# mLSTM heads' ends: squares ahead of the output gate, a root table asked for ahead of its use, and a sixth out-projection tile beside the last head

## The chip, the cores and the metric

The kernel runs on one core of one Trainium2 chip. The metric is the device time of one launch in microseconds (us). The engines are named as in the profile: PE (TensorE, matrix multiplies; its weight loads are PEld), DVE (VectorE), ACT (ScalarE), POOL (GpSimd) and SP (SyncE, which issues most weight loads). Each runs its own instructions in a fixed order and waits on semaphores for the others. What lies in PSUM, where matmuls add up, has names that begin with `p` (`pmm`, `psc`, `ptr`, of which there are three, three and two).

## The reference, cut to what matters

The kernel computes two layers of an encoder on 512 tokens of width 1024. The change lies in the first layer's mixer: four mLSTM heads of width 192 and a memory attention are set side by side, multiplied by one matrix, and added to the input:

```python
hm = mlstm_chunkwise(q, k, v, ig, jax.nn.log_sigmoid(fg))      # num / max(|den|, exp(-m)) per head
hm = hm * lax.rsqrt(jnp.mean(hm * hm, axis=-1, keepdims=True) + EPS)
hm = hm.reshape(bsz, seq, A_WIDTH) * a_head_g[a]
mix_out = (hm * jax.nn.sigmoid(o)).astype(x.dtype)
mem_out = memory_attention(q_mem, mem, mem_w_kv[l])
x = x + jnp.concatenate([mix_out, mem_out], axis=-1) @ a_w_out[a]
x = x + conv_ffn(rmsnorm(x, norm_ffn_g[l]), ...)
```

## The kernel before

All activations lie transposed, 128 features by 512 tokens in a tile. Every float32 operand of a matmul is split into a high part (`split` casts it, ACT, L113) and a low part (the difference, DVE, L114), and each product is three matmuls (`mm3`, L157 to L159: high by high, low by high, high by low in the weights). Weights come from memory in `wr` (SP), and are split into `wh` and `wl`; there are three buffers of each.

`mlstm_head(h)` is a generator. For each of the four blocks of 128 keys it makes weighted scores (the exp of a gate term on ACT, L1136; the scores on PE; their product on DVE, L1142; split to `pt`), and `products` multiplies them by the values into two `ptr` tiles. Then comes the head's end: both tiles are squared on ACT (L1172) and multiplied by the output gate `og` on DVE (L1174); the denominator's floor is added to the squares (L1177, L1178), the sum is split, summed over the features by a matmul with ones (L1186), and a reciprocal square root on ACT (L1188, with its table load, since it lies in another table than exp) with one Newton step on DVE (L1189 to L1191) gives the factor. The gated tiles are multiplied by it (L1194) and split: these are the mixes of the head, operands of the out-projection. Heads 0 to 2 fill mixes 0 to 3 in part, head 3 the mixes 4 and 5; the memory attention gives 6 and 7.

`weave(job, filler, each)` interleaves: for each `yield` of the job (or each unit of `yield 2.6`), `each` steps of the filler are taken. For heads 0 to 2 the filler is projections of the layer's input, for head 3 the out-projection's steps, one `mm3` a step. A scheduler then orders each engine's instructions by its own estimates, so the code's order is not the program's order.

`OutProjection` has the eight output tiles in groups: tiles 0 to 2 in `pmm`, 3 and 4 in `ptr`. `part(g, ks)` loads the weights of group g for the mixes ks and issues one `mm3` for each mix and tile. `finish` goes through all eight tiles: one that no group holds is made by `project` on the spot (24 matmuls, weights of 512 KB), then the residual is added (DVE, L609), the tile written out, its square added up (ACT L245 or L248, DVE L249) and the scaled tile split for the feed-forward network (ACT L285, DVE L286). Its weights follow.

Of the kernel before, what the change touches and what calls it, by code (L numbers as in the profile page):

```python
# [12 lines left out]
AF = mybir.ActivationFunctionType  # L13
ALU = mybir.AluOpType
AX = mybir.AxisListType

P = 128
# [6 lines left out]
AH = 4  # L24
# [22 lines left out]
def f(ap):  # L47
    return ap.bitcast(F32)
# [3 lines left out]
def trunk(  # L52
# [19 lines left out]
    V, A, G = nc.vector, nc.scalar, nc.gpsimd  # L72
# [10 lines left out]
    def sb(tag, shape, dtype=F32):  # L83
        count[0] += 1
        return pool.tile(shape, dtype, tag=tag, name=f"{tag}{count[0]}", bufs=bufs[tag])

    def ps(tag):
        count[0] += 1
        return psum.tile([P, S], F32, tag=tag, name=f"p{tag}{count[0]}", bufs=pbufs[tag])

    def small(n=4):
        return sb("s", [P, 32])[:, :n]
# [4 lines left out]
    ones = cpool.tile([P, P], F32, name="ones")  # L97
# [7 lines left out]
        out=maskf, in_=maskf, pattern=[[1, P]], base=0, channel_multiplier=-1,  # L105
# [6 lines left out]
    def split(hi, lo, src, on_act=True, pinned=False):  # L112
        high = A.copy(hi, src) if on_act else V.tensor_copy(hi, src)  # L113
        low = V.tensor_tensor(out=lo, in0=src, in1=f(hi), op=ALU.subtract)  # L114
        if pinned:
            pin(high)
            pin(low)
# [37 lines left out]
    def mm3(o, lh, ll, rh, rl, first, last, more=False):  # L155

        nc.tensor.matmul(o, lh, rh, start=first, stop=False, skip_group_check=more)  # L157
        nc.tensor.matmul(o, lh, rl, start=False, stop=False, skip_group_check=more)  # L158
        nc.tensor.matmul(o, ll, rh, start=False, stop=last, skip_group_check=more)  # L159
# [13 lines left out]
    def run(gen):  # L173
        while True:
            try:
                next(gen)
            except StopIteration as end:
                return end.value

    def chain(*gens):  # L180
        for g in gens:
            yield from g
# [6 lines left out]
    def weave(job, filler, each, lead=0):  # L189

        due = lead
        for n in chain([0], job):
            due += each if n is None else each * n
            while due >= 1:
                due -= 1
                next(filler, None)
# [293 lines left out]
    def head_scores(o, h, q, tsl, k, c, first, keys_first=False):  # L490

        for i, part in enumerate(q):
            a, b = part[h][:, tsl], k[h][:, c]
            if keys_first:
                a, b = b, a
            nc.tensor.matmul(o, a, b, start=first and i == 0, stop=i == 1)  # L496
# [479 lines left out]
    e, u, c, r = (cpool.tile([P, TT, AH], F32, name=f"gate{i}") for i in range(4))  # L976
# [76 lines left out]
    mixes = [None] * KT  # L1053
# [28 lines left out]
    qs, ks, og = [None] * 6, [None] * 6, [None] * 6  # L1082

    def a_tiles(*js):
        for j in js:
            qs[j] = yield from qk_tile(j)
            ks[j] = yield from qk_tile(6 + j)
        for j in js:
            og[j] = yield from o_tile(j)
# [8 lines left out]
    def exponents(h, s):  # L1098

        n = S - s * P  # L1100
        r = sb("bias", [P, S])
        src = bass.AP(tensor=rowd.tensor, offset=rowd.offset + (s * AH + h) * S + s * P, ap=[[0, P], [1, n]])
        pin(G.dma_start(r[:, :n], src))
        exps[h, s] = r
# [3 lines left out]
    def den_floor(h):  # L1108

        floors[h] = sb("bias", [P, S])  # L1110
        src = bass.AP(tensor=floord.tensor, offset=floord.offset + h * S, ap=[[0, P], [1, S]])
        pin(G.dma_start(floors[h], src))
# [11 lines left out]
    def mlstm_head(h):  # L1124
        hp, odd = divmod(h, 2)
        sh = 3 * hp + 1
        full = 3 * hp + 2 * odd
        rs, ds = HEADS[odd], HEADS[1 - odd]
        pt = sb("pt", [P, 5 * S], F32R)

        def weighted_scores(s):
            n = S - s * P
            sl = slice(s * P, (s + 1) * P)
            r = exps.pop((h, s))
            e = sb("t", [P, S])
            A.activation(e[:, :n], r[:, :n], AF.Exp, bias=acol[:, s, h : h + 1])  # L1136
            yield
            o = ps("sc")
            kf, qf = ks[full], qs[full]
            mm3(o[:, :n], kf[0][:, sl], kf[1][:, sl], qf[0][:, s * P :], qf[1][:, s * P :], True, False)  # L1140
            head_scores(o[:, :n], odd, qs[sh], slice(s * P, S), ks[sh], sl, False, True)
            V.scalar_tensor_tensor(e[:, :n], o[:, :n], DH**-0.5, e[:, :n], op0=ALU.mult, op1=ALU.mult)  # L1142
            split(pt[:, RO[s] : RO[s + 1]], pt[:, 1280 + RO[s] : 1280 + RO[s + 1]], e[:, :n])
            yield

        nums = []

        def products(s):
            if not nums:
                nums.extend(ps("tr") for _ in range(2))  # L1150
            for o, c in zip(nums, (3 * P, 2 * P) if odd else (0, P)):
                mm3(
                    o[:, s * P :], vh[hp][s][:, c : c + P], vl[hp][s][:, c : c + P],
                    pt[:, RO[s] : RO[s + 1]], pt[:, 1280 + RO[s] : 1280 + RO[s + 1]], s == 0, s == TT - 1,
                )
            yield

        yield from weighted_scores(0)
        yield from weighted_scores(1)
        yield from weighted_scores(2)  # L1160
        yield from products(0)
        yield from weighted_scores(3)
        den_floor(h)
        for s in range(TT if h < AH - 1 else 0):
            exponents(h + 1, s)
        yield from products(1)
        yield from products(2)
        yield from products(3)
        sqs = []
        for o, j, r in ((nums[0], full, slice(0, P)), (nums[1], sh, rs)):  # L1170
            sq = sb("t", [P, S])
            A.activation(sq, o, AF.Square)  # L1172
            sqs.append(sq)
            V.tensor_tensor(out=og[j][r, :], in0=o[r, :], in1=og[j][r, :], op=ALU.mult)  # L1174
        yield
        sq, den = sqs
        V.scalar_tensor_tensor(den[ds, :], den[ds, :], EPS * DH / HD, floors.pop(h)[ds, :], op0=ALU.mult, op1=ALU.max)  # L1177
        V.tensor_add(sq, sq, den)  # L1178
        hi, lo = sb("t", [P, S], F32R), sb("t", [P, S], F32R)
        split(hi, lo, sq)  # L1180
        for s in range(TT if h < AH - 1 else 0):
            masked(h + 1, s)
        yield 2.6
        o = ps("sc")
        for i, part in enumerate((hi, lo)):
            nc.tensor.matmul(o, onesr, part, start=i == 0, stop=i == 1)  # L1186
        fb, t = sb("t", [P, S]), sb("t", [P, S])
        A.activation(fb, o, AF.Abs_reciprocal_sqrt, scale=1.0 / DH)  # L1188
        V.tensor_mul(t, fb, fb)  # L1189
        V.scalar_tensor_tensor(t, t, -0.5 / DH, o, op0=ALU.mult, op1=ALU.mult)  # L1190
        V.scalar_tensor_tensor(fb, t, 1.5, fb, op0=ALU.add, op1=ALU.mult)  # L1191
        yield 3.4
        for j, r in ((full, slice(0, P)), (sh, rs)):
            V.tensor_tensor(out=og[j][r, :], in0=fb[r, :], in1=og[j][r, :], op=ALU.mult)  # L1194
            if mixes[j] is None:
                mixes[j] = sb("u", [P, S], F32R), sb("u", [P, S], F32R)
            split(mixes[j][0][r, :], mixes[j][1][r, :], og[j][r, :])

    outp = OutProjection(a_w_out, mixes, (0, 3, "mm"), (3, 5, "tr"))
    run(value_columns(1))  # L1200
    load_vectors(1)
    load_vectors(2)
# [2 lines left out]
    fill = gate_rows()  # L1205
# [6 lines left out]
    fill = chain(a_tiles(2), a_memory_queries(0), a_tiles(3, 4), a_tiles(5), a_memory_queries(1))  # L1212
# [10 lines left out]
    fill = chain(outp.part(0, 0, 1), outp.part(0, 2, 6), outp.part(0, 3))  # L1223
    weave(memory_attention(memq[1], memkv, 1, mixes), fill, 0.475)
    job = mlstm_head(3)
    fill = chain(fill, outp.part(0, 7))
    weave(islice(job, 13), fill, 0.85)
    fill = chain(fill, outp.part(1, 0, 1, 2, 6), outp.part(1, 3, 7))
    weave(job, fill, 0.862)
    run(chain(fill, outp.part(0, 4, 5), outp.part(1, 4, 5)))  # L1230
    norm, (act,) = outp.finish([col["gffn"][:, 0:8]])


# [19 lines left out]
    for j in range(KT):  # L1253
        wh, wl = weights(rows(ffn_w_down[0], j * P, P, FT - LAST, FT), LAST, P)
        o = ps("mm")
# [10 lines left out]
    mixes = [None] * KT  # L1266
# [98 lines left out]
    outp = OutProjection(b_w_out, mixes, (0, 3, "mm"), (3, 5, "sc"))  # L1365
    fill = chain(*(project_pair(j) for j in range(5)), b_memory_queries(0), project_pair(5), b_memory_queries(1))
# [11 lines left out]
    fill = chain(outp.part(0, 0, 1), outp.part(0, 2, 6), outp.part(0, 3, 4))  # L1378
    weave(memory_attention(memq[1], memkv, 1, mixes), fill, 0.48, 4)
    job = band_attention(5, *qkv.pop(5))  # L1380
    fill = chain(fill, outp.part(0, 7))
    weave(islice(job, 8), fill, 2.372)
    fill = chain(fill, outp.part(1, 0, 1, 2, 6), outp.part(1, 3, 4, 7))
# [124 lines left out]
```

## Time and profile before

| | |
|---|---|
| three runs | 1206.86, 1205.56, 1205.6 us; median 1205.6 |
| profiled execution | 1206.7 us, span 1204.9 us, granted PE clock 0.998 in the mean |
| busy: PE, DVE, ACT, POOL | 1185.9, 940.3, 723.1, 145.1 us |
| matmuls `pmm<-u,wh` and `pmm<-u,wl` of 128x512 on L157 to L159 | 968 on each line, 336.3, 333.6 and 333.4 us |
| the stretch 240 to 260 us (head 3's end, out-projection) | PE busy 17.45 of 20.00 us, granted clock 0.91 |
| the stretch 260 to 280 us | PE busy 20.00 of 20.00 us, granted clock 1.00 |

A row of the timeline gives the start in the span, the duration, engine, line, operation, output and inputs, the shape, how many of a kind follow one another, and in brackets the idle time ahead of it with the work that ended it. A matmul's duration includes its fill, so rows overlap; the distance of starts tells the pace. A row of the waits gives who waited for whom, us in total, times, and the longest. A row of a window gives its length, busy time and instructions, the granted clock as a share of full speed, the DMA engines' share and GB/s.

### The profile page before, as it was taken

The numbers are of one execution on the slowest core, as the hardware profiler recorded it, in microseconds if no ns is written. First come the engines' busy times: TensorE is split into PE (matmuls) and PEld (weight loads), VectorE is DVE, ScalarE is ACT, GpSimd is POOL, SyncE is SP. The second block draws the span as 40 slices with busy tenths as digits, with TensorE's granted clock in tenths as the row PEclk, the third lists the DMA queues.
The fourth block names the chain that finished last, engine by engine and source line by source line (L and its number), as shares of the span: only waits on it lengthen the run. The fifth ranks groups of instructions, "written<-read, shape, count | busy, mean of one in ns | idle before, by whom it ended". The sixth has DMA issues, their size and how long they took to land.

```text
span 1204.9 us, 18596 instructions
## 1 busy us (share of the span) xinstructions
PE 1185.9 (98%) x6963; PEld 1048.4 (87%) x6963; DVE 940.3 (78%) x1666; ACT 723.1 (60%) x1266; POOL 145.1 (12%) x234
## 2 busy tenths in 40 slices
PE   9999999999999999999999999999999999999997
PEld 9988888877889999999888888888888999999986
DVE  6877797777978777777698888997896777777755
ACT  4547796654656555555566677775565555555545
POOL 0202201011011111111020000101101010111100
PEclk9999999999999999999999999999999999999999
DMA  8637322448465777665563313244745466666551
GB/s 277 204 103 163 94 73 71 144 139 191 108 155 139 161 163 160 150 145 126 140 205 119 88 56 98 74 141 150 183 105 132 118 130 139 140 141 136 119 157 70
DMA packets 206635, 162.83 MB, mean 135 GB/s; under 512 B 8420, under 2 KB 186058, under 8 KB 206546
## 3 DMA queue, kind: packets, MB, share of 16 engines
q1 hardware_dynamic: 184338, 120.78, 34.2%
q0 software_dynamic: 22208, 40.87, 18.1%
q8 instruction: 54, 0.88, 0.3%
q14 instruction: 35, 0.29, 0.1%
HBM read 133.09 MB, written 32.47 MB: 137 GB/s over the span
## 4 chain that ended last, share of the span: by engine, by line
PE 80%; issue 12%; DVE 2%; DMA 2%; ACT 2%; POOL 1%; POOLq 0%; SPq 0%; ACTq 0%; DVEq 0%
PE pmm L157 15%; PE pmm L159 15%; PE pmm L158 15%; PE ptr L158 5%; PE ptr L157 5%; PE ptr L159 5%; PE psc L159 5%; PE psc L157 4%; PE psc L158 4%; PE psc L496 2%; DMA pt<-in_ffn_w_up_dram 2%; PE ptr L1335 1%; POOL xspill L610 1%; ACT wh L113 0%; PE ptr L1356 0%
## 5 line engine op out<-in xcount | busy, mean ns | idle before, releaser
L157 PE MATMUL pmm<-u,wh 128*128 128x512 f32 (+1 forms) x968 | 336.3, 348 | 2.2 <-ACT u L113 2.1
L158 PE MATMUL pmm<-u,wh 128*128 128x512 f32 (+1 forms) x968 | 333.6, 345 | 0.0
L159 PE MATMUL pmm<-u,wl 128*128 128x512 f32 (+1 forms) x968 | 333.4, 345 | 0.0
L114 DVE TENSOR_TENSOR wl<-wr,wh 128x1024 fp32r<-128x1024 f32 (+4 forms) x168 | 194.5, 1158 | 96.5 <-ACT wh L113 95.5
L113 ACT CAST wh<-wr 128x1024 fp32r<-128x1024 f32 (+4 forms) x168 | 167.9, 1000 | 93.9 <-PE pmm L158 44.5
L157 PEld LDWEIGHTS pmm<-u,wh 128*128 128x128 f32 x968 | 183.9, 190 | 21.2 <-ACT u L113 3.1
L159 PEld LDWEIGHTS pmm<-u,wl 128*128 128x128 f32 x968 | 183.9, 190 | 21.1
L158 PEld LDWEIGHTS pmm<-u,wh 128*128 128x128 f32 x968 | 184.1, 190 | 18.2 <-DVE u L114 0.2
L157 PE MATMUL ptr<-u,wh 128*128 128x512 f32 x272 | 106.8, 394 | 0.0
L158 PE MATMUL ptr<-u,wh 128*128 128x512 f32 x272 | 106.5, 392 | 0.0
L159 PE MATMUL ptr<-u,wl 128*128 128x512 f32 x272 | 105.8, 389 | 0.0
L727 POOL DMA_DIRECT2D xspill<-t x64 | 56.0, 875 | 408.1 <-ACT t L726 399.0
L157 PE MATMUL pmm<-u,u 128*128 128x256 f32 x296 | 84.5, 285 | 2.8 <-ACT t L803 2.8
L159 PE MATMUL pmm<-u,u 128*128 128x256 f32 x296 | 84.0, 284 | 0.4 <-DVE u L114 0.4
L158 PE MATMUL pmm<-u,u 128*128 128x256 f32 x296 | 83.8, 283 | 0.0
L114 DVE TENSOR_TENSOR u<-pt,u 128x512 fp32r<-128x512 f32 x102 | 69.8, 687 | 9.7 <-ACT u L113 7.1
L726 ACT COPY t<-ptr 128x512 f32<-128x512 f32 x64 | 37.5, 586 | 65.4 <-PE ptr L159 65.4
L157 PE MATMUL psc<-u,wh 128*128 128x256 f32 (+1 forms) x232 | 76.1, 328 | 0.0
L158 PE MATMUL psc<-u,wh 128*128 128x256 f32 (+1 forms) x232 | 75.9, 327 | 0.0
L114 DVE TENSOR_TENSOR u<-t,u 128x512 fp32r<-128x512 f32 x78 | 53.3, 688 | 22.6 <-ACT u L113 22.2
L113 ACT CAST u<-pt 128x512 fp32r<-128x512 f32 x102 | 63.0, 618 | 11.4 <-DVE pt L838 11.2
L900 ACT ACTIVATE t<-t 128x512 f32<-128x512 f32 x34 | 21.5, 633 | 80.2 <-DVE t L636 80.2
(281 smaller groups left out, 2557.2 us busy)
## 6 DMA issues: line engine op xcount, KB each, us to landing
wr<-in_ffn_w_up_dram SPq DMA_DIRECT2D x54, 512.0 KB, 4.4
wr<-in_ffn_w_down_dram SPq DMA_DIRECT2D x38, 512.0 KB, 3.8
pt<-in_ffn_w_up_dram SPq DMA_DIRECT2D x34, 512.0 KB, 6.6
xspill<-t POOLq DMA_DIRECT2D x64, 256.0 KB, 4.9
wr<-in_a_w_in_dram SPq DMA_DIRECT2D x20, 512.0 KB, 3.9
xspill<-u POOLq DMA_DIRECT2D x32, 256.0 KB, 2.9
u<-xspill SPq DMA_DIRECT2D x32, 256.0 KB, 5.1
wr<-in_w_kv_dram SPq DMA_DIRECT2D x12, 512.0 KB, 4.0
```

Of the source, the lines that this page charges most:

```text
L113: high = A.copy(hi, src) if on_act else V.tensor_copy(hi, src)
L114: low = V.tensor_tensor(out=lo, in0=src, in1=f(hi), op=ALU.subtract)
L157: nc.tensor.matmul(o, lh, rh, start=first, stop=False, skip_group_check=more)
L158: nc.tensor.matmul(o, lh, rl, start=False, stop=False, skip_group_check=more)
L159: nc.tensor.matmul(o, ll, rh, start=False, stop=last, skip_group_check=more)
L496: nc.tensor.matmul(o, a, b, start=first and i == 0, stop=i == 1)
L610: pin(G.dma_start(xspill[j], xT[j]))
L726: A.copy(t, o)
L727: G.dma_start(xspill[j], t, accum_op=ALU.add)
L900: A.activation(self.acc, self.acc, AF.Silu)
L1335: nc.tensor.transpose(tp[:, b * P : (b + 1) * P], es[T, h][:, b * P : (b + 1) * P], ident)
```

## The change

In every head the squares of both tiles are issued ahead, and the multiplies by the output gate come behind the split of the sum. The filler ahead of the ones-matmul grows (`yield 3.6` for 2.6). Head 3 computes a reciprocal square root of a column of ones behind its split, whose result nobody reads. The out-projection has a third group, tile 5 alone in `psc`, whose parts for mixes 0, 1, 2, 6, 3 and 7 join the filler of head 3, with 1.4 steps a yield for 0.862, and whose parts 4 and 5 come behind those of the other groups. So `finish` makes tiles 6 and 7 on the spot, where it made 5, 6 and 7. Lines of the changed kernel: L1176, L1177 for the floor and the sum (L1177, L1178 before), L1181 for the gate (L1174), L1185 for the new root, L1189 for the ones-matmul (L1186), L1191 to L1194 for the root (L1188 to L1191), L1197 for the mixes (L1194).

```diff
@@ mlstm_head
-        for o, j, r in ((nums[0], full, slice(0, P)), (nums[1], sh, rs)):
+        for o in nums:
             sq = sb("t", [P, S])
             A.activation(sq, o, AF.Square)
             sqs.append(sq)
-            V.tensor_tensor(out=og[j][r, :], in0=o[r, :], in1=og[j][r, :], op=ALU.mult)
         yield
...
         split(hi, lo, sq)
+        for o, j, r in ((nums[0], full, slice(0, P)), (nums[1], sh, rs)):
+            V.tensor_tensor(out=og[j][r, :], in0=o[r, :], in1=og[j][r, :], op=ALU.mult)
         for s in range(TT if h < AH - 1 else 0):
             masked(h + 1, s)
-        yield 2.6
+        if h == AH - 1:
+            A.activation(small(1), ones[:, :1], AF.Abs_reciprocal_sqrt)
+        yield 3.6
...
-    outp = OutProjection(a_w_out, mixes, (0, 3, "mm"), (3, 5, "tr"))
+    outp = OutProjection(a_w_out, mixes, (0, 3, "mm"), (3, 5, "tr"), (5, 6, "sc"))
...
-    fill = chain(fill, outp.part(1, 0, 1, 2, 6), outp.part(1, 3, 7))
-    weave(job, fill, 0.862)
-    run(chain(fill, outp.part(0, 4, 5), outp.part(1, 4, 5)))
+    fill = chain(fill, outp.part(1, 0, 1, 2, 6), outp.part(1, 3, 7), outp.part(2, 0, 1, 2, 6, 3, 7))
+    weave(job, fill, 1.4)
+    run(chain(fill, outp.part(0, 4, 5), outp.part(1, 4, 5), outp.part(2, 4, 5)))
```

The matmuls are as many as before, 6944. DVE has one instruction more, and ACT four (the new root, one cast more of weights, two table loads more: 27 for 25). On SP one load of 512 KB (the weights of tile 5) becomes eight of 64 KB.

Where the instructions stand now, at four places. First ACT, from the memory attention's last casts (`pt`, L113) to head 3's first exps (L1136). Before:

```order
L553 ACTIVATE t_2395,s_2393<-psc_2368,s_2392 128x256 x2
L113 CAST pt_2324<-ptr_2401 128x2x256
L113 CAST pt_2325<-ptr_2411 128x2x256
L113 CAST pt_2324<-ptr_2418 128x2x256
L113 CAST pt_2325<-ptr_2428 128x2x256
L113 CAST wh_2605<-wr_2600 128x1024
L515 COPY t_2449<-ptr_2435 64x512
L515 COPY t_2449<-ptr_2443 64x512
L1136 ACTIVATE t_2469<-bias_2143,acol 128x512
```

And now:

```order
L113 CAST pt_2325<-ptr_2411 128x2x256
L113 CAST wh_2567<-wr_2565 128x384
L1185 ACT_TABLE_LOAD
L1185 ACTIVATE s_2598<-ones 128x1
L113 CAST pt_2324<-ptr_2418 128x2x256
L113 CAST pt_2325<-ptr_2428 128x2x256
L515 COPY t_2449<-ptr_2435 64x512
L1136 ACT_TABLE_LOAD
L1136 ACTIVATE t_2469<-bias_2143,acol 128x512
L515 COPY t_2449<-ptr_2443 64x512
```

The new root and its table load have moved up into the memory attention, and a load of exp's table follows ahead of the head's scores. Second PE, around head 3's ones-matmuls (`onesr`), with the out-projection's filler about them. Before:

```order
L159 MATMUL ptr_2598<-u_1521,wl_2606 128x512
L1186 MATMUL psc_2615<-t_2594,onesr 128x512
L157 MATMUL ptr_2599<-u_1521,wh_2605 128x512
L158 MATMUL ptr_2599<-u_1522,wh_2605 128x512
L159 MATMUL ptr_2599<-u_1521,wl_2606 128x512
L1186 MATMUL psc_2615<-t_2595,onesr 128x512
```

And now:

```order
L159 MATMUL ptr_2600<-u_1762,wl_2608 128x512
L1189 MATMUL psc_2626<-t_2592,onesr 128x512
L1189 MATMUL psc_2626<-t_2593,onesr 128x512
L157 MATMUL ptr_2601<-u_1762,wh_2607 128x512
L158 MATMUL ptr_2601<-u_1763,wh_2607 128x512
```

The two parts of the sum now follow each other, and fifteen matmuls of filler stand between the head's last products and them, where nine stood ahead of the first. Third PE, where tile 6 (`pmm_2803` before, `pmm_2817` now, with the weights `wh_2799`, `wl_2800` and `wh_2813`, `wl_2814`) begins. Before:

```order
L159 MATMUL pmm_2763<-u_2454,wl_2760 128x512
L157 MATMUL pmm_2803<-u_1516,wh_2799 128x512
L158 MATMUL pmm_2803<-u_1517,wh_2799 128x512
L159 MATMUL pmm_2803<-u_1516,wl_2800 128x512
L157 MATMUL pmm_2803<-u_1521,wh_2799 128x512
```

And now:

```order
L159 MATMUL psc_2671<-u_2655,wl_2749 128x512
L157 MATMUL pmm_2817<-u_1519,wh_2813 128x512
L158 MATMUL pmm_2817<-u_1520,wh_2813 128x512
L157 MATMUL pmm_2857<-u_1519,wh_2853 128x512
L158 MATMUL pmm_2857<-u_1520,wh_2853 128x512
L157 MATMUL pmm_2898<-u_2762,wh_2894 128x512
L158 MATMUL pmm_2898<-u_2763,wh_2894 128x512
L159 MATMUL pmm_2817<-u_1519,wl_2814 128x512
```

Before, tile 5's 24 matmuls (`pmm_2763`) ran ahead of tile 6; now the last six of tile 5 (`psc_2671`), and then the high halves of tile 6, of tile 7 and of the network's first tile (`pmm_2898`). Fourth DVE, the same place. Before, behind the first three residuals:

```order
L609 TENSOR_TENSOR u_2314<-u_2314,ptr_2598 128x512
L609 TENSOR_TENSOR u_2316<-u_2316,ptr_2599 128x512
L114 TENSOR_TENSOR wl_2800<-wr_2797,wh_2799 128x1024
L249 TENSOR_TENSOR rb_2715<-rb_2715,t_2741 128x512
L286 SCALAR_TENSOR_TENSOR u_2745<-u_2314,cols_519,u_2744 128x512
```

And now:

```order
L609 TENSOR_TENSOR u_2314<-u_2314,ptr_2600 128x512
L609 TENSOR_TENSOR u_2316<-u_2316,ptr_2601 128x512
L609 TENSOR_TENSOR u_2318<-u_2318,psc_2671 128x512
L249 TENSOR_TENSOR rb_2760<-rb_2760,t_2786 128x512
L286 SCALAR_TENSOR_TENSOR u_2790<-u_2314,cols_519,u_2789 128x512
L249 TENSOR_TENSOR rb_2760<-rb_2760,t_2795 128x512
L286 SCALAR_TENSOR_TENSOR u_2799<-u_2316,cols_519,u_2798 128x512
L249 TENSOR_TENSOR rb_2760<-rb_2760,t_2804 128x512
L114 TENSOR_TENSOR wl_2814<-wr_2811,wh_2813 128x1024
```

The low half of tile 6's weights stood behind five residuals; it now stands behind six, and behind the norm sums and scalings of tiles 3 and 4 too.

## The prediction

> **What bounds the kernel now.** I read the page's first two parts, the list of waits, and then the timeline of TensorE (PE) over the four heads' ends, with DVE and ACT beside it.
>
> ```profile
> span 1204.9 us, 18596 instructions
> PE 1185.9 (98%) x6963; PEld 1048.4 (87%) x6963; DVE 940.3 (78%) x1666; ACT 723.1 (60%) x1266; POOL 145.1 (12%) x234
> ```
>
> PE is busy for 98% of the span and no other engine for more than 78%. The change leaves the number of matmuls as it was, so it can move the time only by taking holes out of PE's stream or putting new ones in. The profiled execution took 1206.7 us; the three runs have a median of 1205.6, so I sum against 1206.7 and take 1.1 off at the end. What differs from the time before by 0.2%, 2.4 us, or less cannot be told from no change.
>
> What the holes cost is read from starts: PE's rows start one pace apart while it streams.
>
> ```profile
> 259.42 0.39 PE L157 MATMUL pmm<-u,wh 128*128 128x512 f32 x1
> 261.46 0.39 PE L157 MATMUL pmm<-u,wh 128*128 128x512 f32 x1
> ```
>
> Nine rows lie between these two, all of one kind: 2.04 us / 9 = 0.227 us a matmul. A start that comes later than that has lost the excess. The waits that touch the stage of the change:
>
> ```profile
> PE pmm L157 <- ACT u L113: 2.1, 1, 2.1
> PE psc L1186 <- ACT t L113: 1.5, 4, 0.4
> ```
>
> The second is each head's end: the matmul by ones (L1186) waits for the cast of the summed squares. The rows just ahead of each and it:
>
> ```profile
> 128.64 0.39 PE L158 MATMUL pmm<-u,wh 128*128 128x512 f32 x1
> 129.27 0.50 PE L1186 MATMUL psc<-t,onesr 128*128 128x512 f32 x1 [0.24 <-ACT t L113]
> 129.61 0.40 PE L159 MATMUL pmm<-u,wl 128*128 128x512 f32 x1
> ...
> 150.60 0.39 PE L159 MATMUL pmm<-u,wl 128*128 128x512 f32 x1
> 151.43 0.50 PE L1186 MATMUL psc<-t,onesr 128*128 128x512 f32 x1 [0.44 <-ACT t L113]
> ...
> 206.53 0.39 PE L158 MATMUL pmm<-u,wh 128*128 128x512 f32 x1
> 207.28 0.50 PE L1186 MATMUL psc<-t,onesr 128*128 128x512 f32 x1 [0.36 <-ACT t L113]
> ...
> 241.03 0.40 PE L159 MATMUL ptr<-u,wl 128*128 128x512 f32 x1
> 241.87 0.50 PE L1186 MATMUL psc<-t,onesr 128*128 128x512 f32 x1 [0.44 <-ACT t L113]
> ```
>
> Start to start less the pace: 0.40, 0.60, 0.52 and 0.61 us, and the matmul behind starts 0.34 instead of 0.23 after it, 0.11 more each time. So the four ends cost 0.51, 0.71, 0.63 and 0.72 us. Head 3 has the large hole too, where the out-projection needs the last head's mixes:
>
> ```profile
> 248.39 0.39 PE L159 MATMUL ptr<-u,wl 128*128 128x512 f32 x1
> 250.89 1.61 PE L157 MATMUL pmm<-u,wh 128*128 128x512 f32 x3 [2.11 <-ACT u L113]
> ```
>
> The windows (PE's busy time and instructions, granted clock, DMA share, GB/s):
>
> ```profile
> 39.34:42.75 3.41, 1.96 (x11) 1.00 0.35 78
> 42.75:46.16 3.41, 3.37 (x19) 1.00 0.93 266
> 247.55:250.96 3.41, 1.30 (x7) 1.00 0.51 154
> 250.96:254.38 3.42, 3.42 (x8) 0.50 0.51 152
> ```
>
> From 248.39 to 250.89 are 2.50 us, less one pace 2.27 us of wait. Behind the window with 1.30 us of work PE ran 3.42 us at clock 0.50, eight matmuls where fifteen fit, 3.42 - 8 x 0.227 = 1.6 us lost; with the ramp's edges I take 1.7. A window with 1.96 us of work elsewhere was followed by full clock, so the limit lies between the two.
>
> The Trainium skill ("TensorE: Matmul & The Clock Gate", Part 1) puts the drop behind an idle window of some 3.4 us. Here a wait of 2.27 us was enough, in a window that was 38% busy; by the page a new hole of this size would cost no clock, by the row it does, and I go by the row.
>
> **The change part by part.** *Squares ahead, og multiplies behind the split, heads 0 to 2.* The number of DVE operations does not change. The order of the two kernels shows DVE with the same four operations ahead of the cast in heads 0 and 1 and one multiply less in head 2, and PE with the ones-matmul later by 1 matmul (head 0) and 3 (head 1), and two places earlier in head 2, 0.23 us each. One multiply of the gate takes this long:
>
> ```profile
> 148.59 0.69 DVE L1174 TENSOR_TENSOR u<-ptr,u 64x512 f32<-64x512 f32 x1
> ```
>
> Head 0: 0.51 - 0.23, and the low half no longer splits PE's stream, 0.1 left. Head 1: 0.71 - 0.69 for three matmuls, but its low half is due right behind and DVE's taps stand ahead of it, 0.35 left. Head 2: 0.63 - 0.69 + 0.46, 0.45 left. Gain 0.51 + 0.71 + 0.63 - 0.90 = 0.9 (0.95, taken down). Ends: 0.4 if the scheduler's other moves (convolution taps put ahead of the low half in heads 0 and 1) make the low half late, 1.8 if all goes.
>
> *Head 3's root (yield 3.6, denser filler).* The ones-matmul now stands 15 matmuls behind the products instead of 9: 6 x 0.23 = 1.4 us later against a wait of 0.61, and its low half follows directly, due as the DVE row ends.
>
> ```profile
> 241.20 0.62 ACT L113 CAST t<-t 128x512 fp32r<-128x512 f32 x1 [1.21 <-DVE t L1178]
> 241.90 0.69 DVE L114 TENSOR_TENSOR t<-t,t 128x512 fp32r<-128x512 f32 x1
> 243.38 1.28 ACT L1188 ACT_TABLE_LOAD   x1 [1.56 <-PE psc L1186]
> ```
>
> Gain 0.7 (0.4 to 0.72).
>
> *The root's table, "early".* It does not come early in the order. The dummy's load and ACTIVATE (L1185) stand between the memory attention's casts, a third load brings exp back for head 3's scores, and the real root (L1191) still has its own load behind its wait on PE. So the load of 1.28 us at 243.38 stays in the chain and two more are issued, 2.57 us of ACT, in a stretch where it waits now and then:
>
> ```profile
> 226.00 0.59 ACT L113 CAST pt<-ptr 128x512 fp32r<-128x512 f32 x1 [1.42 <-PE ptr L565]
> 230.34 1.63 ACT L1136 ACTIVATE t<-bias,acol 128x512 f32<-128x512 f32 x3
> 231.35 0.39 PE L159 MATMUL pmm<-u,wl 128*128 128x512 f32 x1
> 232.19 0.33 PE L157 MATMUL psc<-u,u 128*128 128x128 f32 x1 [0.46 <-DVE t L1142]
> ```
>
> The scores of head 3 lose 0.84 - 0.23 = 0.61 at 232.19 now, for the exp that started at 230.34. In the new order the exps alternate with the casts they feed, and two filler matmuls more stand ahead of the last score. Walking the queues row by row I get a gain of 0.5 in this stretch; the ends are a gain of 0.9 (such waits gone, the 0.61 and what the casts behind it lose) and a loss of 2.57 (both loads on the path). The Trainium skill ("ScalarE: Activation LUTs", What ACT_TABLE_LOAD costs) has a switch at 2.66 us with its drain; the row has 1.28, and by the page's price, an estimate, this end would be 2.8 us deeper.
>
> *Tile 5 beside head 3.* Its 18 matmuls stand between the ones-matmuls and the first use of a mix. From the low half's start the mixes took 250.89 - 242.91 = 8.0 us, an ACT cast in between that waited for PE included:
>
> ```profile
> 242.91 0.39 PE L1186 MATMUL psc<-t,onesr 128*128 128x512 f32 x1
> 248.63 1.04 ACT L113 CAST wh<-wr 128x1024 fp32r<-128x1024 f32 x1 [2.14 <-PE ptr L158]
> 250.85 1.41 DVE L114 TENSOR_TENSOR u<-u,u 128x512 fp32r<-128x512 f32 x2
> ```
>
> Now 39 matmuls lie between the low half and that use, 39 x 0.227 = 8.8 us. The wait of 2.27 goes and with it the clock drop of 1.7. Gain 4.0; the cover is thin for the second low half, so 3.5 at the lower end.
>
> *What tile 5 no longer covers.* Behind its parts PE now issues three pairs by high halves (tiles 6, 7 and the FFN's first), and then stands at tile 6's low half, `wl_2814`. On DVE that split waits behind the residuals, norm sums and scalings of six tiles; before, behind ten such operations, with tile 5's 24 matmuls to hide them:
>
> ```profile
> 255.99 2.05 DVE L609 TENSOR_TENSOR u<-u,pmm 128x512 f32<-128x512 f32 x3 [3.74 <-PE pmm L159]
> 257.99 0.75 DVE L286 SCALAR_TENSOR_TENSOR u<-u,cols,u 128x512 fp32r<-128x512 f32 x1
> 258.66 0.68 DVE L249 TENSOR_TENSOR rb<-rb,t 128x512 f32<-128x512 f32 x1
> 261.19 1.28 DVE L609 TENSOR_TENSOR u<-u,ptr 128x512 f32<-128x512 f32 x2
> 262.38 1.22 DVE L114 TENSOR_TENSOR wl<-wr,wh 128x1024 fp32r<-128x1024 f32 x1
> ```
>
> From the first residual to that split's start: 262.38 - 255.99 = 6.39 us for 10 operations, 0.64 each and back to back. Now there are 16 (6 + 5 + 5): 10.2 us, and 1.22 for the split: ready 11.45 us after the first residual. PE at that time has 29 matmuls left ahead of the low half (5 of tiles 1 and 2, 12 of tiles 3 and 4, 6 of tile 5, 6 high halves): 29 x 0.227 = 6.6 us. The hole is 4.9 us, in two pieces, since the last of the three pairs waits for ACT's cast behind the same work. Ends: 3.9 if DVE's operations overlap better, 5.5.
>
> A hole of 4.9 us is longer than the window that dropped the clock. Shared evenly by two windows it leaves each at least 2.4 us without work, less busy than the 1.96 us that kept the clock, so I expect a drop. What it costs hangs on the phase: 0.5 if most of the slow window is still hole, 1.7 for one full, 2.2 for one and a part. I take 1.4.
>
> *Loads and the rest.* One load of 512 KB becomes eight of 64 KB on SP; casts of tile 5's weights are now three. They run ahead by three buffers beside PE's fill and cost nothing; if one were late it would be a wait like the row at 248.63, at most its own 1 us. What follows (norm's sums, FFN's weights) depends on PE's and DVE's end here and shifts with them.
>
> Sum: -0.9 - 0.7 - 0.5 - 4.0 + 4.9 + 1.4 = +0.2 us: 1206.9 for the profiled execution, 1205.8 beside the median.
>
> **The rivals.** *As its words say (faster).* The hole at 250.89 goes and none comes: if the split of tile 6 were not late, because DVE had the residuals of the early tiles done while PE streams, the sum would be -6.1: 1199.5. For it speaks that DVE waits 3.74 us ahead of 255.99; against it that no residual can be added before its tile's last mix, so the ten operations cannot move ahead. Between the two lies a smaller hole (3.9) without a clock drop: -0.9 - 0.7 - 0.5 - 4.0 + 3.9 = -2.2, and with 0.4 more from the heads -2.6: 1203.0.
>
> *The table loads land on the path (slower).* The second extra load stands directly ahead of head 3's first exp, and PE waits for the scores made from it already. If ACT has no idle time there to take the two loads, the stretch loses 2.57 us instead of gaining 0.5: +0.2 + 3.1 = +3.3, 1208.9. The idle of 1.42 us before 226.00 speaks against it; it decides from the point where ACT, with the loads, still works on the casts `pt` when PE reaches the first products, some 1.4 us of delay onward.
>
> *The new hole costs two slow windows.* 2.6 instead of 1.4 us: +1.4, 1207.0, within the same bound.
>
> *No drop behind the new hole.* If only a window wholly without work drops the clock, the hole's pieces of about 3.2 and 1.1 us cost none: +0.2 - 1.4 = -1.2, 1204.4, within the same bound. One pair of rows, 247.55 and 250.96, speaks against it and none for it. (This is the rule of the Trainium skill's page on TensorE named above.)
>
> *The table loaded early after all.* If the early load served the root, 1.28 us would leave the mixes' chain; since the 39 matmuls cover that chain anyway, the sum would not change.
>
> **How the numbers follow.** The forecast, a new hole that gives back what the old one cost, has 0.58, the version without a drop (0.1) and that with two (0.1) in it. A smaller hole without a drop, at about 1203, has 0.14; the words' version 0.10 at 1199.5; the loads on the path 0.10 at 1208.9; several terms at their bad ends together 0.08, above that. All good ends of the terms but no missing hole: -1.8 - 0.7 - 0.9 - 4.0 + 3.9 + 0.5 = -3.0, 1202.6; all bad ones: -0.4 - 0.4 + 2.6 - 3.5 + 5.5 + 2.2 = +6.0, 1211.6. The range 1202.0 to 1209.2 takes in the first and reaches to the loads' rival, and leaves out the words' version (0.10) and the worst sums (0.06). Faster by over 0.2% (below 1203.2): 0.24; within: 0.58; slower (above 1208.0): 0.18.
>
> **What would show it.** In the new profile: no wait of `L157 pmm` for ACT's `u` ahead of the mixes and full clock there; head 3's ones-matmul without a wait; 27 table loads, one of them of L1185 among the memory attention's casts; and, as the sign of the forecast, a wait of PE at L159 for DVE's `wl` (and two matmuls ahead of it one at L157 for ACT's cast), 4 to 5 us in all, six high halves behind tile 5's end, with a window of lower clock behind it. If that wait is missing I am wrong by the terms 4.9 and 1.4, and the kernel is faster by 6 us; if PE waits more than now at head 3's scores, by the term 0.5.

## The result, and the profile after

The changed kernel took 1210.54 us in the median of six runs (1209.01 to 1211.74), the kernel before 1206.16 beside it: a ratio of 1.0035 (95% interval 1.0024 to 1.0047), 4.2 us slower, where 0.2 us more was forecast. The profiled execution is the quickest of the six. Its PE has as many instructions as before, 6963.

```profile
span 1207.1 us, 18613 instructions
PE 1187.3 (98%) x6963; PEld 1047.2 (87%) x6963; DVE 940.3 (78%) x1667; ACT 725.1 (60%) x1270; POOL 146.6 (12%) x234
```

The waits of PE that are new or longer, from the list of waits after:

```profile
PE pmm L157 <- ACT wh L113: 4.6, 3, 3.0
PE pmm L159 <- DVE wl L114: 0.9, 1, 0.9
PE psc L1189 <- DVE t L114: 0.5, 2, 0.3
PE ptr L157 <- ACT pt L113: 0.4, 1, 0.4
PE psc L1189 <- ACT t L113: 0.2, 1, 0.2
```

The wait `PE pmm L157 <- ACT u L113` of 2.1 us is gone, the first line has grown from 1.4 us (one wait) to 4.6 (three), and the fourth from 0.2 to 0.4. PE's timeline shows where the largest are, behind the last matmul of tile 5 (`psc`):

```profile
260.69 0.39 PE L159 MATMUL psc<-u,wl 128*128 128x512 f32 x1
260.92 0.49 PE L157 MATMUL pmm<-u,wh 128*128 128x512 f32 x1
261.25 0.40 PE L158 MATMUL pmm<-u,wh 128*128 128x512 f32 x1
261.85 0.50 PE L157 MATMUL pmm<-u,wh 128*128 128x512 f32 x1 [0.21 <-ACT wh L113]
262.19 0.40 PE L158 MATMUL pmm<-u,wh 128*128 128x512 f32 x1
265.58 0.50 PE L157 MATMUL pmm<-u,wh 128*128 128x512 f32 x1 [3.00 <-ACT wh L113]
265.93 0.39 PE L158 MATMUL pmm<-u,wh 128*128 128x512 f32 x1
267.24 0.79 PE L159 MATMUL pmm<-u,wl 128*128 128x512 f32 x1 [0.92 <-DVE wl L114]
267.83 0.63 PE L157 MATMUL pmm<-u,wh 128*128 128x512 f32 x1
```

Seven starts between 260.69 and 267.24 would take 7 x 0.227 = 1.59 us; they take 6.55. The hole is 4.96 us, against 4.9 forecast. The work that it waits for, on DVE:

```profile
255.68 2.05 DVE L609 TENSOR_TENSOR u<-u,pmm 128x512 f32<-128x512 f32 x3 [2.04 <-PE pmm L159]
...
262.07 0.68 DVE L609 TENSOR_TENSOR u<-u,psc 128x512 f32<-128x512 f32 x1
...
265.37 0.68 DVE L249 TENSOR_TENSOR rb<-rb,t 128x512 f32<-128x512 f32 x1
265.97 1.22 DVE L114 TENSOR_TENSOR wl<-wr,wh 128x1024 fp32r<-128x1024 f32 x1
```

From the first residual to the split's start are 265.97 - 255.68 = 10.29 us for 16 operations (forecast 10.2), DVE without a gap. Behind the hole the clock drops, in the windows of that execution (PE busy, granted clock, DMA share, GB/s):

```profile
263.42:266.83 3.41, 0.73 (x2) 1.00 0.49 179
266.83:270.25 3.42, 3.01 (x7) 0.50 0.50 149
270.25:273.66 3.41, 3.41 (x16) 1.00 0.90 257
```

The heads' ends, just ahead of the ones-matmul and at it:

```profile
129.15 0.39 PE L157 MATMUL pmm<-u,wh 128*128 128x512 f32 x1
129.69 0.50 PE L1189 MATMUL psc<-t,onesr 128*128 128x512 f32 x1 [0.15 <-DVE t L114]
...
153.50 0.39 PE L157 MATMUL pmm<-u,wh 128*128 128x512 f32 x1
154.21 0.50 PE L1189 MATMUL psc<-t,onesr 128*128 128x512 f32 x1 [0.31 <-DVE t L114]
...
206.37 0.39 PE L159 MATMUL pmm<-u,wl 128*128 128x512 f32 x1
206.98 0.50 PE L1189 MATMUL psc<-t,onesr 128*128 128x512 f32 x1 [0.22 <-ACT t L113]
```

Less the pace they lose 0.31, 0.48 and 0.38 us, with 0.11 behind each; before it was 0.40, 0.60 and 0.52. In heads 0 and 1 it is now the sum's low half, DVE's, that PE waits for.

To see where all of it went I took from the timelines the start of PE's n-th matmul and subtracted that of the kernel before; both have issued the same number by then, and the start of the stage (the 700th) is taken as zero. A positive number is time lost. In us:

| kernel | behind head 2 (1200th) | behind head 3's products (1255th) | among the mixes (1325th) | in tile 7 and the network's first tile (1400th) |
|---|---|---|---|---|
| changed | +0.77 | +0.73 | -3.76 | +2.75 |
| e3, heads' order only | +0.75 | -0.29 | -0.15 | -0.15 |
| g4, the same with yield 2.6 | +0.37 | -0.66 | -0.73 | -0.73 |
| f3, early root only | -0.02 | +0.70 | -0.15 | -0.15 |
| e4, tile 5 only | -0.03 | -0.04 | -4.05 | +3.01 |
| e2, changed without the early root | +0.72 | -0.31 | -4.71 | +2.95 |
| e1, changed, tiles 6 and 7 first | +0.76 | +0.74 | -3.78 | -3.78 |
| g2, e1 without the early root | +0.79 | -0.26 | -4.63 | -4.63 |

The first column hangs on its place, since the kernels issue the matmuls of this stretch in different orders. From the 1110th to the 1138th, just behind head 2's sum, it would read +0.54 to +0.56 for the changed kernel, +0.51 to +0.53 for e3 and +0.04 to +0.06 for g4; at the 1220th, ahead of head 3's first scores, +0.87, +0.84 and +0.46.

So the changed kernel loses 0.77 over heads 0 to 2 (0.54 to 0.87 by the place), nothing at head 3's products, wins 4.49 at the mixes, and loses 6.51 at the new hole.

### The profile page after: what moved, and what is told of

Same layout as the page of the kernel before. It is cut to its first block, busy times and chain, and to the rows that moved or that the text cites. A ratio compares the mean times of both kernels' runs of the same rounds, so it can differ in the third digit from the quotient of the medians.

```text
span 1207.1 us, 18613 instructions
## 1 busy us (share of the span) xinstructions
PE 1187.3 (98%) x6963; PEld 1047.2 (87%) x6963; DVE 940.3 (78%) x1667; ACT 725.1 (60%) x1270; POOL 146.6 (12%) x234
## 4 chain that ended last, share of the span: by engine, by line
PE 77%; issue 12%; DVE 3%; ACT 3%; DMA 3%; POOL 1%; SPq 0%; POOLq 0%; ACTq 0%; DVEq 0%
PE pmm L157 15%; PE pmm L158 14%; PE pmm L159 14%; PE ptr L157 5%; PE ptr L158 5%; PE ptr L159 5%; PE psc L159 5%; PE psc L157 4%; PE psc L158 4%; DMA pt<-in_ffn_w_up_dram 2%; PE psc L496 2%; PE ptr L1338 1%; POOL xspill L610 1%; DVE t L1063 1%; PE ptr L1359 0%
## 5 line engine op out<-in xcount | busy, mean ns | idle before, releaser
L157 PE MATMUL pmm<-u,wh 128*128 128x512 f32 (+1 forms) x960 | 333.2, 347 | 3.3 <-ACT wh L113 3.2
L114 DVE TENSOR_TENSOR wl<-wr,wh 128x1024 fp32r<-128x1024 f32 (+2 forms) x169 | 194.5, 1153 | 95.9 <-ACT wh L113 95.6
L113 ACT CAST wh<-wr 128x1024 fp32r<-128x1024 f32 (+2 forms) x169 | 167.7, 995 | 100.2 <-PE pmm L158 47.6
L157 PEld LDWEIGHTS pmm<-u,wh 128*128 128x128 f32 x960 | 182.6, 190 | 22.6 <-ACT wh L113 4.3
L157 PE MATMUL ptr<-u,wh 128*128 128x512 f32 x272 | 106.7, 392 | 0.0
L157 PE MATMUL pmm<-u,u 128*128 128x256 f32 x296 | 84.5, 285 | 2.5 <-ACT t L803 2.5
L157 PE MATMUL psc<-u,wh 128*128 128x256 f32 (+1 forms) x240 | 79.2, 330 | 0.0
L158 PE MATMUL psc<-u,wh 128*128 128x256 f32 (+1 forms) x240 | 79.0, 329 | 0.0
L113 ACT CAST u<-pt 128x512 fp32r<-128x512 f32 x102 | 63.0, 617 | 11.7 <-DVE pt L838 11.7
```

## The experiments

Theory A: the loss is the new hole in front of tile 6's low half and the slow clock behind it. Theory B: the two table loads and the new order at the heads cost it.

**e1: tiles 6 and 7 first.** In `OutProjection.finish`:

```diff
             for j in range(KT):
-                o = self.o[j] if j in self.o else run(project(self.w, j * P, self.mixes))
+                if j not in self.o:
+                    self.o[j] = run(project(self.w, j * P, self.mixes))
+            for j in range(KT):
+                o = self.o[j]
                 V.tensor_add(xT[j], xT[j], o)
```

> The changed kernel, with finish issuing the products of tiles 6 and 7 ahead of all residuals, so that tile 6's low half stands behind three residuals on DVE instead of behind sixteen operations. Theory A (the loss is the new hole of 5.0 us in front of tile 6's low half and the slow clock behind it, 1.5 us in the profiled run and more in others): hole and slow window gone, 5 to 8 us less than the changed kernel, 1202.5 to 1205.5, so faster than the kernel before by 1 to 3.5 us. Theory B (the two extra table loads and the new order at the heads' ends cost the time): no more than 1 us less than the changed kernel, 1209 to 1210.5.

1202.6 us in the median of 5 runs, ratio to the kernel before 0.9962 (0.995 to 0.9975): 4.6 us faster, more than the 1 to 3.5 expected. Its DVE and PE at the same place:

```profile
255.50 2.05 DVE L612 TENSOR_TENSOR u<-u,pmm 128x512 f32<-128x512 f32 x3 [2.04 <-PE pmm L159]
257.83 1.22 DVE L114 TENSOR_TENSOR wl<-wr,wh 128x1024 fp32r<-128x1024 f32 x1 [0.28 <-ACT wh L113]
...
260.52 0.39 PE L159 MATMUL psc<-u,wl 128*128 128x512 f32 x1
260.74 0.39 PE L157 MATMUL pmm<-u,wh 128*128 128x512 f32 x1
260.97 0.39 PE L158 MATMUL pmm<-u,wh 128*128 128x512 f32 x1
261.20 0.39 PE L159 MATMUL pmm<-u,wl 128*128 128x512 f32 x1
```

The split follows three residuals instead of sixteen operations and ends at 259.05, two microseconds before PE needs it at 261.20; PE runs through. The residuals and norm sums run beside the 48 matmuls of tiles 6 and 7. The table's last column falls from +2.75 to -3.78: the hole and its clock were 6.5 us of the profiled execution. Theory A holds, theory B alone cannot give this.

**e2: no early root.** The two lines `if h == AH - 1:` and `A.activation(small(1), ...)` out.

> The changed kernel without the root of a column of ones (and so without the two table loads more). Theory A: within 1 us of the changed kernel, 1209.5 to 1211; the hole of 5 us stands. Theory B: 2 to 2.6 us less than the changed kernel, about 1208, and the wait of 0.57 us at head 3's first products gone.

1209.36 us (11 runs), ratio 1.0015 (1.0006 to 1.0024). The median lies between what theory A and theory B expected, 1.2 us below the changed kernel's. The runs alone do not decide between them. In the trace the hole stands, as theory A has it, and the early root's 1.0 us is gone at head 3's products (+0.73 to -0.31). In the table's last column this gain is hidden by the clock, which was at half for two windows behind the hole instead of one.

**e3: the heads' order alone.** The out-projection as before, no early root.

> Only the new order of the heads' ends (squares ahead, gate behind the split, yield 3.6); no new root, no tile 5. Theory A: the wait ahead of the mixes (2.3 us) and its slow window stay as before, the ones-matmul of head 3 gains up to 0.6, heads 0 to 2 nothing: 1205 to 1207. Theory B: slower than before by 1 to 2 us, 1207 to 1208.

1206.83 us (11 runs), ratio 0.9995 (0.9986 to 1.0004). As theory A has it: no measurable difference. It loses 0.75 over heads 0 to 2 and wins 1.04 at head 3's products; the wait ahead of the mixes is there, 2.27 us as before.

**e4: tile 5 alone.** The third group, its parts and the 1.4 steps on top of the kernel before.

> Only the sixth out-projection tile beside head 3 (with 1.4 steps a yield), heads' ends as before. Theory A: the old hole of 2.3 us and its slow window gone, the new hole of 5 us and its slow windows there: like the changed kernel within 1.5 us, 1209 to 1212. Theory B: no extra loads and no new order at the heads, so no slower than before, 1203 to 1206.

1210.07 us (11 runs), ratio 1.0026 (1.0017 to 1.0035). Within the noise the whole loss is there with tile 5 alone. Its windows show the clock at half for two windows on end:

```profile
261.53:264.94 3.41, 1.36 (x5) 1.00 0.32 112
264.94:268.35 3.41, 1.62 (x3) 0.50 0.33 124
268.35:271.77 3.42, 3.42 (x9) 0.50 0.60 175
```

Behind the first, with 1.36 us of work, the second is at half clock; the second has the rest of the hole in it, and behind it the third is at half clock too, in which PE has full work. What the hole costs through the clock thus hangs on how it lies across the windows, and I set out to price that.

**f1 and f2: the hole filled.** f1 is the changed kernel again. In f2 tile 6's first matmul is issued twelve times more, into the same accumulator, which each starts anew; PE has them to do while it would stand idle.

```diff
+        for _ in range(again):
+            nc.tensor.matmul(o, wh[:, 0, :], act[0][0], start=True, stop=False, skip_group_check=True)
         for k in range(n):
             mm3(o, wh[:, k, :], wl[:, k, :], act[k][0], act[k][1], k == 0, k == n - 1)
...
-                o = self.o[j] if j in self.o else run(project(self.w, j * P, self.mixes))
+                o = self.o[j] if j in self.o else run(project(self.w, j * P, self.mixes, again=12 if j == 6 else 0))
```

> The changed kernel once more, for the comparison with the three kernels beside it on the same chip: 1209 to 1212 by both theories.

> The changed kernel with tile 6's first matmul issued thirteen times instead of once (each starts the sum anew, so the result is the same); the twelve more run in the time in which PE stands in the hole, which keeps its length. Theory A (behind the hole of 5 us PE runs one or two windows of 3.4 us at half clock, the second wherever the first is itself nearly empty): the granted clock stays at 1.00 there and the kernel takes 1.5 to 3 us less than the changed one, 1207 to 1209, with less spread between its runs, although PE has 12 matmuls more to do. Theory C (the slow windows cost little, since the same waits would have followed): no difference, 1210 to 1211.

f1 took 1210.93 us (5 runs), ratio 1.003 (1.0018 to 1.0043), f2 1211.79 (6 runs), 1.004 (1.0028 to 1.0052). f2 is inconclusive by my own edit: the second layer's out-projection has a tile 6 too, and there the twelve matmuls, at 833 us, had no hole to run in and cost their 2.7 us.

**g1: the hole filled in the first layer alone** (`again=12 if j == 6 and 5 in self.o else 0`).

> As f2_hole_filled, whose twelve extra matmuls ran in the second layer's out-projection too, where no hole is and they cost 12 x 0.227 = 2.7 us; here they run in the first layer's hole alone. Theory A: 1211.8 - 2.7 = 1209.1 (1208 to 1209.5), 1.5 to 2.5 us less than the changed kernel, at full granted clock behind the hole. Theory C (slow windows cost little): 1210.5 to 1211.

1207.8 us (11 runs), ratio 1.0015 (1.0006 to 1.0024). PE at the hole:

```profile
261.21 3.00 PE L169 MATMUL pmm<-u,wh 128*128 128x512 f32 x12
...
265.89 0.50 PE L157 MATMUL pmm<-u,wh 128*128 128x512 f32 x1 [0.78 <-ACT wh L113]
...
267.55 0.50 PE L159 MATMUL pmm<-u,wl 128*128 128x512 f32 x1 [0.92 <-DVE wl L114]
267.89 0.39 PE L157 MATMUL pmm<-u,wh 128*128 128x512 f32 x1
```

Tile 6's low half is taken up at 267.55, as late as in the changed kernel (267.24), and yet the kernel is quicker, though it has more to do: the next start comes 0.34 us later instead of 0.59, at full clock. The profiled execution has no window at half clock here. Counted at the 1400th matmul, g1's twelve more left out, it stands at +1.29, where the changed kernel with one slow window stands at +2.75 and f1 with two at +3.51: 1.5 and 2.2 us for the clock. In the runs the gain over f1 is 0.0015 by the two ratios, 1.8 us, and 3.1 by the medians; these kernels ran at different times and the two intervals overlap, so the size is rough. Theory C falls by the traces, and the median is 0.2 below theory A's range.

**f3: the early root alone**, on the kernel before.

> The kernel before with nothing but the root of a column of ones in head 3, which the scheduler sets among the memory attention's casts, with two table loads more. Theory A: these loads push the exps and casts of head 3's first products, 0.5 to 1.5 us more than before. Theory C (ACT has idle time there): no more than 0.2 us more.

1208.47 us (11 runs), ratio 1.0013 (1.0005 to 1.0022), 1.6 us slower. ACT and PE:

```profile
225.13 1.28 ACT L1184 ACT_TABLE_LOAD   x1
...
230.76 1.28 ACT L1136 ACT_TABLE_LOAD   x1
232.06 0.72 ACT L1136 ACTIVATE t<-bias,acol 128x512 f32<-128x512 f32 x1
...
233.34 0.72 PE L157 MATMUL pmm<-u,wh 128*128 128x512 f32 x2 [1.18 <-ACT u L113]
```

The second load pushes head 3's first exp from 230.34 to 232.06; as all rows of this execution lie some 0.54 us later here, that is 1.2 us, and PE waits 1.18 us for a cast behind it. The first load lies in ACT's idle time: the cast behind it starts at 226.54, where 226.00 and the 0.54 stand before. So about one of the two loads is on the path. In this profiled execution no slow window came behind the wait at the mixes (2.36 us here), which is why the table has f3 level again in its third column; the runs were 1.6 us slower. The windows there:

```profile
248.23:251.64 3.41, 1.51 (x7) 1.00 0.49 149
251.64:255.05 3.41, 2.47 (x9) 1.00 0.30 89
```

**f4: the root late enough.** e3 with the new root reading the head's own split sum, `A.activation(small(1), f(hi)[:, :1], AF.Abs_reciprocal_sqrt)`, so that it cannot be moved ahead of it.

> The heads' new order alone (as in the run of heads only), with the new root reading a column of head 3's split sum, so that it cannot move ahead of it: its table load stands behind the cast and the real root has none. Theory A: the load of 1.28 us leaves the chain to the mixes, the wait of 2.27 us there shrinks to 1.0 to 1.5 and leaves its window busy enough, so no slow window: 2.5 to 3 us less than heads only, 1203 to 1204.5. Theory C (the chain is held by ACT's casts of weights, not by the load): at most 0.5 us less, 1206 to 1207.

1203.9 us (7 runs), ratio 0.9974 (0.9963 to 0.9985). ACT:

```profile
240.73 0.62 ACT L113 CAST t<-t 128x512 fp32r<-128x512 f32 x1 [1.36 <-DVE t L1177]
241.36 1.28 ACT L1185 ACT_TABLE_LOAD   x1
242.66 0.20 ACT L1185 ACTIVATE s<-t 128x1 f32<-128x1 f32 x1
242.88 0.60 ACT L1191 ACTIVATE t<-psc 128x512 f32<-128x512 f32 x1
```

The load runs while PE sums the squares, and the root follows right behind the small one, 0.24 us behind the load's end; in e3 it came at 244.40, behind a load that itself waited for PE until 243.11. The mixes are there in time: no wait of PE over 0.4 us is left at this place, not even the 1.0 that was expected, because the two casts of the mixes now also go ahead of a cast of weights that waits for PE. This is the change's second idea at work, with the order of the casts: together they are worth 2.5 us beside e3 by the ratios and 2.9 by the medians (1203.9 for 1206.83). The casts of the mixes come 2.86 us earlier (246.41 for 249.27); the root comes 1.52 earlier, and the rest is the cast of weights that stood ahead of them in e3. So f4 does not separate the load from the casts, which theory C named.

**g2 and g3: what to keep.** g2 is e1 without the early root; g3 is e4 with tiles 6 and 7 first (the heads' ends as before).

> Tiles 6 and 7 ahead of the residuals, and no early root. Theory A (the hole and its slow windows are 6.5 to 7.7 us, the early root 1.0 us, and the terms add): 1 us less than e1, 1201.6 (1201 to 1202.2). Theory C (the early root's delay is taken up later): 1202.6 as e1.

> Tile 5 beside head 3 and tiles 6 and 7 ahead of the residuals, the heads' ends as before (no new order, no new root). Theory A (the heads' new order loses 0.7 us over heads 0 to 2 and wins 1.0 at head 3's first products and 0.4 at its ones-matmul): 0.7 us more than g2, 1202.3 (1201.8 to 1203). Theory D (the new order is what the rest needs): 1203.5 or more.

g2 took 1201.53 us (5 runs), ratio 0.9962 (0.995 to 0.9975), 4.6 us faster than the kernel before, the lowest median of all; g3 1202.93 (6 runs), 0.9969 (0.9957 to 0.9981). The early root's delay is there in the table's third column (-3.78 to -4.63, 0.85 us); between the ratios of e1, g2 and g3 the runs cannot decide.

**g4: the heads' order with the filler of before** (`yield 2.6`).

> The heads' new order with the filler of before (yield 2.6). If the denser filler is what lost 0.7 us over heads 0 to 2: PE is level with the kernel before when head 2 is over (within 0.2 us), 1205.5 to 1206.5. If the order of squares and gate is what lost it: 0.7 us behind there as in e3, 1206.5 to 1207.5.

1205.72 us (11 runs), ratio 0.9993 (0.9984 to 1.0001). Halfway at the 1200th, +0.37 for +0.75; just behind head 2's sum it is level, as the first expectation has it. At head 1's end (the 845th matmul) g4 and e3 are level, both some 0.25 ahead of the kernel before. At the 1040th, among head 2's blocks, g4 still is, and e3 is 0.45 behind: so the denser filler costs 0.7 there. At head 2's sum the sparser one waits 0.83 for the ones-matmul and gives some of that back:

```profile
206.47 0.50 PE L1187 MATMUL psc<-t,onesr 128*128 128x512 f32 x1 [0.67 <-ACT t L113]
```

## Why the prediction was wrong

It forecast no change and named the right mechanism for the largest terms, and failed by two terms of its sum and one that it sized for one window.

- *Heads 0 to 2, -0.9 forecast, +0.77 measured (+0.54 just behind head 2's sum).* This is the step that failed: a gain was forecast and a loss came. The ones-matmul was placed later as read from the order, but the waits at it went from 1.85 us to 1.78 only (the three starts above, 0.11 behind each, and 0.27 at head 2's low half), since the low half behind convolution taps on DVE became what PE waits for; the prediction had that as the lower end, a gain of 0.4. It also took head 0's low half as no longer splitting PE's stream and head 1's as due right behind the high one; in the changed kernel's rows one and seven matmuls of filler stand between, and PE waits at both. The rest, 0.6 us just behind head 2's sum, is nearly all two pauses between the ends of heads 1 and 2, 0.25 and 0.32 us with the slower start behind each, where a weight load waits for ACT (rows below). Neither pause is in g4, so the new place of the filler makes them; the prediction's sum had no term for what the filler does there. I looked at the places where PE waited and not at those where it now would. What makes the smaller pauses behind head 2 is not settled.
- *Head 3's products, -0.5 forecast, -0.04 measured.* The order of the heads gives the gain (-1.04 in e3), and the early root takes it back (1.0 us in e2 at this place, 0.7 in f3, 0.85 between e1 and g2 at the mixes). The rival of the loads had the place right; its price, both loads on the path, was too high, since one found idle time.
- *Root and mixes, -4.7 forecast, -4.49 measured.* Right: the 39 matmuls cover the mixes, the clock stays up there. In the rows 20 matmuls, not 15, stand between head 3's products and its sum, where 15, not 9, stood before; five more are enough, and the sum has no wait.
- *The new hole, +4.9 forecast, 4.96 measured.* Right to the operation: ten became sixteen, at 0.64 us each, and 29 matmuls stand between the first residual and the low half in the rows too.
- *The slow clock behind it, +1.4 forecast.* 1.5 us in the profiled execution, which had one slow window; in the runs 1.8 to 3.1 (g1). The profiled executions of e2, e4 and f1, with the same hole, had two slow windows each. The mean granted clock, 0.998 in the profiled execution and 0.995 to 0.997 in the five other runs, points the same way without showing it for each. The prediction had two windows as a rival, at 2.6, with a chance of 0.1; of the four profiled executions, one has a single slow window. That 1.4 fits the profiled execution is thus luck in part.

The two pauses between the ends of heads 1 and 2, in the changed kernel's weight loads:

```profile
167.33 0.54 PEld L496 LDWEIGHTS psc<-u,u 128*128 128x128 f32 x4 [0.41 <-ACT t L553]
192.02 0.30 PEld L157 LDWEIGHTS ptr<-pt,u 128*128 128x128 f32 x2 [0.47 <-ACT pt L113]
```

The profiled execution adds up: 0.77 - 0.04 - 4.49 + 6.51 = +2.75, where the prediction had +0.2. The rest of the 4.2 us, 1.4, fits a second slow window in most of the runs, and is not shown run by run. Either error alone, the heads' or the second window's, would have left the time below the range's upper end, 1209.2.

The prediction's reading that the limit of the clock lies between 1.30 and 1.96 us of work does not hold as a single limit: 1.51 kept the clock in f3, and 1.93 lost it in g3. The Trainium skill ("TensorE: Matmul & The Clock Gate", Part 1) puts the drop behind an idle window of some 3.4 us. This case does not bear that out: windows with 1.36 us of work (e4) and 1.93 (g3) were followed by half clock.

## What to carry to other kernels

A block of work that is moved to fill one hole was covering something where it stood: look up what the next queue does in its place, here the operations ahead of one DVE split, and issue that split first (e1, some 8 us beside the changed kernel). Work that is meant to come "early" needs a dependence that holds it in place, or a scheduler may put it where it costs. A hole of PE of about 5 us is better priced with two slow windows behind it: three of the four profiled executions with this hole had two.

## What the hardware showed that I had not expected

The second slow window. At half clock PE needs about twice the time for a matmul (the kernel before has eight in 3.42 us, 0.43 us each, for 0.227). Yet a window with 2.48 us of such work, five matmuls, was followed by another slow one, and so was one with 2.73 us in e2, where 3.01 us, seven matmuls, was not. From f1, to be read beside the changed kernel's windows above:

```profile
262.10:265.51 3.41, 0.72 (x2) 1.00 0.58 211
265.51:268.92 3.41, 2.48 (x5) 0.50 0.09 31
268.92:272.33 3.41, 3.41 (x9) 0.50 0.79 226
```

And at full clock the work in a window does not settle it alone: 1.96 us kept the clock in the kernel before and 1.51 in f3 at the mixes, and 1.93 lost it in g3, at a place near 41 us that no edit touched:

```profile
40.89:44.30 3.41, 1.93 (x9) 1.00 0.47 123
44.30:47.71 3.41, 3.41 (x12) 0.50 0.93 287
```

What else decides is open; the busy time of a window rests on modelled ends of matmuls.

The same hole lies differently across the windows from one execution to the next: f1 is the changed kernel again, and there a window ends at 265.51, 2.15 us ahead of tile 6's low half (267.66); in the first execution one ends at 266.83, 0.41 ahead of it (267.24). That the runs of a kernel with a hole scatter more for it is not shown: the kernel before has 1205.14 to 1209.58 in 27 runs and g2, without the waits at the mixes and behind tile 5, 1201.13 to 1202.41 in 5, but g1 with the hole filled has 1207.17 to 1210.69 in 11.
